# A one-core encoder kernel: plain one-hot products in PSUM, finer background steps in the first mixer, 68 early tiles

## The chip, the cores and the metric

The kernel runs on one core of one Trainium2 chip. The metric is device time in microseconds of one execution. Before the change the median of three runs is 3347.67 us (3344.97 to 3349.91).

## The reference, cut to what matters

512 tokens of width 1024 pass through two layers. Layer 0 has an mLSTM mixer with 8 heads, layer 1 a stick-breaking attention with 16 heads; after each mixer comes a PEER expert feed-forward. Every sub-layer is normed, shifted and scaled by vectors that come from a condition c, and its result is gated by another such vector:

```python
sh1, sc1, g1, sh2, sc2, g2 = jnp.split(ada_mod(c, ada_w[layer], ada_b[layer]), 6, axis=-1)
h = modulate(rmsnorm(x, norm_mix_g[layer]), sh1, sc1)
...
x = x + g1[:, None, :] * y
h = modulate(rmsnorm(x, norm_ffn_g[layer]), sh2, sc2)
x = x + g2[:, None, :] * peer_ffn(h, peer_w_q[layer], peer_sub_keys[layer], peer_u[layer], peer_v[layer])
```

In the feed-forward each token picks, for each of 8 heads, 16 of 16384 experts (an expert is a pair of two keys out of 128 each), with softmax weights g. It then adds up g * gelu(u . x) * v over the 128 picks:

```python
u = jnp.take(peer_u, expert, axis=0)
act = jax.nn.gelu(jnp.einsum('thkd,td->thk', u, xb).astype(jnp.float32), approximate=False)
vv = jnp.take(peer_v, expert, axis=0)
return jnp.einsum('thk,thkd->td', (g * act).astype(xb.dtype), vv)
```

## The kernel before, in words

**Products.** All large products take float32 operands split into a rounded high part and a remainder (`whi`, `wlo`), three matmuls for one. ScalarE casts the high part, VectorE or GpSimd subtracts.

**The feed-forward (`peer`, line 763).** 128 tokens gather their experts' rows by indirect DMA. For the other 384 tokens the kernel goes through all 16384 experts densely, in 128 tiles of 128 experts. A tile needs the activations gelu(U x), which are 24 matmuls of 384 columns, the matrix G of routing weights for that tile, and the product with V, which is 18 matmuls of 512 columns.

**The placement stage (lines 808 to 984).** It makes G from one-hot vectors, chunk by chunk: 8 tokens make a chunk (`CHUNK`), and the 384 tokens of a layer make 48 chunks, in two layers 96. For each chunk `expand` (line 919) lets VectorE write the one-hot columns `oA` (line 930) and `oB` (931), GpSimd scale `oA` by the high part of the weight (`oH`, line 933, 8 operations of 128 columns), and three engines share the scaling by the remainder (`oL`): tokens below `SHARE[0]` on GpSimd (935), from there to below `SHARE[1]` on ScalarE (`scale`, 942), the rest on VectorE (937). One chunk later `place` (944) multiplies, two float16 matmuls per token (950 and 951), 16 per chunk, into a PSUM tile `gps` that holds four tokens interleaved, so that one token's 128 results are 4 elements apart. ScalarE copies each four tokens to `stg` (953), whence G goes to DRAM. Between the placements TensorE works on activation tiles that are wanted later: the first `NPRE` = 64 tiles are done here (`early_acts`, 836, matmuls in 845), their count per half chunk given by `share` (962). The first 16 of these stay in SBUF, the rest go to DRAM (855). In this stage the order of TensorE, VectorE and ScalarE is the program's (864).

**The value stage (lines 986 to 1083).** For each of 128 tiles it adds the product with V (1080). Tiles that were not early get their activations here (`act`, 1027, matmuls in 1034). Groups of four early and four late tiles alternate (991 to 997). The gathers of the 128 tokens (1002 to 1022), 257 steps, are spread over the late tiles' steps (1025 and 1073): 64 - 1 - 3 = 60 steps.

**The first mixer (`mlstm`, line 254) and the background sums.** The vectors from c are sums over 8 weight tiles of 512 KB each: VectorE multiplies a tile by c and adds it (`part`, lines 148 and 152), and at the end TensorE adds across partitions by 8 matmuls of one column (`end`, 157). Those not wanted at once are `background` steps. `tick(n)` (89) runs n of them; before each it issues the load of the next one. The tiles live in `araw`, 2 buffers, loaded on the SP queue, which also loads the projections' weights (103). A sum's `end` comes six steps after its last part, or right behind it where `flush` is set (169); in the first mixer this holds for the fourth and for the last sum. The steps run two at a time in the projections (lines 348 and 369) and four at a time at the start of each of the 8 heads (436). A head has four score blocks; for each, VectorE, ScalarE and GpSimd make the weights (`weights_of`, 414, result P of line 428), TensorE fills in with some matmuls of the output gate (`gate`, 442, line 382) and multiplies by P (446). In the heads the order of TensorE alone is the program's (432); elsewhere in the mixer, and on the other engines in the heads, the order is the scheduler's.

Of the kernel before, what the change touches and what calls it, by code (L numbers as in the profile page):

```python
# [7 lines left out]
F32 = mybir.dt.float32  # L8
# [4 lines left out]
AF = mybir.ActivationFunctionType  # L13
# [14 lines left out]
NSUB = ND // 32  # L28
NGRP = NA // 4
GROW = NSUB * 128 + 32  # L30
NPRE = 64
RCHUNK = 2.0
KEEP = (4, 4)
DEPTH = 3
SHARE = (2, 4)
GSTEP = (6, 5, 4, 3, 2)
HLB = 3
CHUNK = 8
# [11 lines left out]
def body(tc, nc, A, ctx):  # L50
# [38 lines left out]
    def tick(n):  # L89
        for _ in range(min(n, len(background))):  # L90
            load, run = background.pop(0)
            load()
            if background:
                background[0][0]()
            run()

    def split(hi, lo, src, eng):
# [37 lines left out]
    def ada(j, ap, pool, ring=None, flush=False):  # L135
        def start():
            acc[j] = pool.tile([128, 1024], F32, name="acc", bufs=2)

        raw = {}

        def load(k):
            if k not in raw:
                raw[k] = ring[k % len(ring)] if ring else pool.tile([128, 1024], F32, name="araw", bufs=2)
                nc.sync.dma_start(raw[k], ap[k])

        def part(k):
            if k == 0:
                first = V.tensor_scalar(acc[j], raw[k], csil[:, 0:1], None, op0=OP.mult)
                if j in (2, 8):
                    tc.keep_in_program_order(first)  # L150
            else:
                V.scalar_tensor_tensor(acc[j], raw[k], csil[:, k:k + 1], acc[j], op0=OP.mult, op1=OP.add)

        def end():
            ps = pp()
            for k in range(KD):
                PE.matmul(ps[:, k:k + 1], acc[j][:, k * 128:(k + 1) * 128], ones[:, 0:1], start=True, stop=True)
            V.tensor_tensor(mod[:, j], ps[:, 0:KD], adab[:, j], op=OP.add)
            if j in scale_of:
                gain(scale_of[j], j)  # L160

        def step(k):
            def run():
                if k == 0:
                    start()
                part(k)
                if k == KD - 1:
                    ends.append(end)
                if ends and (k == 5 or k == KD - 1 and flush):
                    ends.pop(0)()  # L170
            return lambda: load(k), run
        return [step(k) for k in range(KD)]
# [81 lines left out]
    def mlstm():  # L254
        with ExitStack() as st:
# [138 lines left out]
            with tc.tile_pool(name="mlps", bufs=1, space=PSUM) as pq:  # L394
                dn = pq.tile([64, T], F32, name="dn")

                def totals(h, *srcs):
                    for i, src in enumerate(srcs):
                        PE.matmul(dn[32 * i:32 * i + 32], oc[:, 32 - h:64 - h], src, start=h == 0, stop=h == 7)

                def rows_of(h):
                    rb = pq.tile([128, T], F32, name="rb", bufs=2)
                    PE.matmul(rb, sel[:, h], rw, start=True, stop=True)
                    return rb

                def scores_of(h, I):
                    e, r0 = h // 2, 64 * (h % 2)
                    rows = slice(r0, r0 + 64)
                    sp = pq.tile([128, T], F32, name="sp", bufs=2)
                    PE.matmul(sp[:, I * 128:T], qk[4 + e][rows, I * 128:I * 128 + 128], qk[e][rows, I * 128:T],  # L410
                              start=True, stop=True)
                    return sp

                def weights_of(h, I, rb, sp):
                    lo, s = I * 128, slice(I * 128, T)
                    Dm = wk.tile([128, T], F32, name="Dm")
                    for J in range(I, 4):
                        js = slice(J * 128, (J + 1) * 128)
                        n = pairs.index((I, J))
                        if I == J:  # L420
                            V.tensor_scalar(Dm[:, js], rb[:, js], cols[:, n, h:h + 1], 0.0, op0=OP.add, op1=OP.min)
                            S.activation(Dm[:, js], Dm[:, js], AF.Exp)
                        else:
                            S.activation(Dm[:, js], rb[:, js], AF.Exp, bias=cols[:, n, h:h + 1])
                    G.affine_select(Dm[:, lo:lo + 128], Dm[:, lo:lo + 128], pattern=[[1, 128]], compare_op=OP.is_ge,
                                    fill=0.0, base=0, channel_multiplier=-1)
                    Pm = wk.tile([128, T], F32, name=f"P{min(I, 1)}")
                    V.scalar_tensor_tensor(Pm[:, s], sp[:, s], 0.125, Dm[:, s], op0=OP.mult, op1=OP.mult)
                    return Pm

                ms = ExitStack()
                ms.enter_context(tc.manual_schedule(engines={nc.tensor.engine}))
                rb = rows_of(0)
                late = None
                for h in range(8):
                    tick(4)
                    pn = pq.tile([128, T], F32, name="pn")
                    sps = [scores_of(h, 0), scores_of(h, 1)]
                    P0 = None
                    for I in range(4):  # L440
                        Pm = weights_of(h, I, rb, sps[I])
                        gate(GSTEP[I])
                        if I == 0 and late:
                            totals(h - 1, *late)
                        s = slice(I * 128, T)
                        PE.matmul(pn[:, s], vt[I][:, h * 128:(h + 1) * 128], Pm[:, s], start=I == 0, stop=I == 3)
                        if I < 2:
                            sps.append(scores_of(h, I + 2))
                        if I == 0:
                            P0 = Pm  # L450
                        else:
                            G.tensor_tensor(P0[:, s], P0[:, s], Pm[:, s], op=OP.add)
                    if h < 7:
                        rb = rows_of(h + 1)
                    gate(GSTEP[4])
                    S.copy(num[h], pn)
                    sq = wk.tile([128, T], F32, name="cv")
                    S.activation(sq, num[h], AF.Square)
                    late = P0, sq
                gate(4)  # L460
                totals(7, *late)
                gate(24 * 8)
                ms.close()
                rows2 = keep.tile([8, 2, T], F32, name="rows2")
                S.activation(rows2[:, 0], dn[0:8], AF.Abs)
                V.tensor_copy(rows2[:, 1], dn[32:40])
                pd = pp()
                for i in range(2):
                    for J in range(4):
                        PE.transpose(pd[:, i * 32 + J * 8:i * 32 + J * 8 + 8], rows2[:, i, J * 128:(J + 1) * 128], ident[0:8, 0:8])  # L470
                dm = keep.tile([128, 4, 8], F32, name="dm")
                V.tensor_tensor(dm.rearrange("p a b -> p (a b)"), pd[:, 0:32], cols[:, 10:14].rearrange("p a b -> p (a b)"), op=OP.max)
                V.scalar_tensor_tensor(dm, dm, EPS, dm, op0=OP.mult, op1=OP.mult)
                d2 = dm.rearrange("p a b -> p (a b)")
                V.scalar_tensor_tensor(d2, pd[:, 32:64], 1.0 / 128.0, d2, op0=OP.mult, op1=OP.add)
                V.tensor_scalar(dm, dm, 1e-37, None, op0=OP.max)
                S.activation(dm, dm, AF.Sqrt)
                V.reciprocal(dm, dm)
                for h in range(8):
                    S.activation(og[h], og[h], AF.Sigmoid)  # L480
                    V.scalar_tensor_tensor(num[h], og[h], hg[:, h:h + 1], num[h], op0=OP.mult, op1=OP.mult)
# [281 lines left out]
    def peer(l):  # L763
# [3 lines left out]
        with ExitStack() as st:  # L767
# [19 lines left out]
            with ExitStack() as s1:  # L787
# [156 lines left out]
                def place(s, c, stg, oB, oA, oH, oL, gl, o):  # L944

                    for j in range(CHUNK // 4):
                        gps = pq.tile([128, 128, 4], F32, name="gps", bufs=2)
                        for i in range(4):
                            n = 4 * j + i
                            PE.matmul(gps[:, :, i], oB[:, n], oH[:, n], start=True, stop=False)  # L950
                            PE.matmul(gps[:, :, i], oB[:, n], oL[:, n], start=False, stop=True)  # L951
                        k = c * CHUNK + 4 * j
                        S.activation(stg[:, :, k:k + 4], gps, AF.Copy, scale=1.0 / GSCALE)
                    if c == 32 // CHUNK - 1:
                        nc.scalar.dma_start(Gd[:, :, s * 128:(s + 1) * 128].rearrange("g p c -> p g c"),
                                            stg.rearrange("p (g a) t -> p g (a t)", a=4))
# [245 lines left out]
```

## Time and profile before

| | us |
|---|---|
| median of three runs | 3347.67 |
| the profiled execution, its time | 3354.71 |
| its span on the core | 3353.0 |
| first mixer's heads, from to | 195 to 350 |
| placement stages | 580 to 900, 2220 to 2550 |
| value stages | 900 to 1700, 2550 to 3350 |

The span is what the profiler saw of the core; the time has 1.7 us around it. Times in the rows are from the start of the span. PE is TensorE's matmuls, PEld its weight loads, DVE is VectorE, ACT ScalarE, POOL GpSimd, SP the queue that issues loads. A matmul's duration is not its share of the engine, since matmuls overlap: the distance from one start to the next is.

### The profile page before, as it was taken

What the parts mean: (1) busy time and instruction counts of PE and PEld (TensorE: products, weight loads), DVE (VectorE), ACT (ScalarE), POOL (GpSimd) and SP (SyncE); (2) the same over time, 40 slices, a digit from 0 to 9 for tenths busy, and PEclk for the clock granted to TensorE, in tenths of its full rate; (3) what the DMA queues carried; (4) which work ended last, traced back from release to release, by engine and by line L of the source; (5) the groups of instructions that cost most, each with busy time, mean ns of one, the idle gap of its engine ahead of it and who ended that gap; (6) DMA issues with size and microseconds to landing.
All of it is one profiled execution on the core that took longest, in us unless ns stands there. A gap on an engine that the chain in (4) does not pass through costs nothing. (4 is left out here: it accounts for less than half of the span.)

```text
span 3353.0 us, 45548 instructions
## 1 busy us (share of the span) xinstructions
PE 3209.6 (96%) x16160; PEld 2752.9 (82%) x16160; DVE 2468.6 (74%) x4656; ACT 1341.9 (40%) x2090; POOL 1641.2 (49%) x1801
## 2 busy tenths in 40 slices
PE   6879998999999999999989999989999999999999
PEld 5744787999988888888866657889998888888887
DVE  6854379776588888888875483896775887887888
ACT  4234333555433333333342463345553333333332
POOL 3422442888734434444453455258884444344443
PEclk9977999999999999999989899999999999999999
DMA  5653222666799999999956102236668999999997
GB/s 196 210 192 107 69 78 76 189 191 205 219 359 332 336 357 332 341 356 340 335 180 214 57 1 78 70 120 197 206 200 289 338 336 355 335 341 351 338 352 275
DMA packets 306580, 792.41 MB, mean 236 GB/s; under 512 B 24368, under 2 KB 135216, under 8 KB 306352
## 3 DMA queue, kind: packets, MB, share of 16 engines
q1 hardware_dynamic: 120112, 451.83, 38.1%
q0 software_dynamic: 73728, 268.47, 22.0%
q10 hardware_dynamic: 112512, 69.21, 7.1%
q8 instruction: 126, 2.06, 0.2%
q14 instruction: 102, 0.84, 0.1%
HBM read 718.12 MB, written 71.30 MB: 235 GB/s over the span
## 5 line engine op out<-in xcount | busy, mean ns | idle before, releaser
L98 ACT CAST whi<-wraw 128x1024 fp32r<-128x1024 f32 x481 | 504.1, 1050 | 665.2 <-PE y L1080 245.4
L1004 POOL DMA_INDIRECT rows<-in_v,pidx x256 | 360.8, 1409 | 426.0 <-DVE yt L1022 385.9
L99 DVE TENSOR_TENSOR wlo<-wraw,whi 128x1024 fp32r<-128x1024 f32 x384 | 469.3, 1222 | 130.1 <-ACT whi L98 129.1
L1004 POOL DMA_INDIRECT rows<-in_u_rows,pidx x256 | 319.0, 1246 | 483.8 <-DVE rows L1011 427.1
L933 POOL TENSOR_SCALAR oH<-oA,gh 128x128 f16<-128x128 f16 x768 | 440.7, 588 | 229.1 <-DVE oA L930 190.2
L1080 PE MATMUL y<-wlo,Wh 128*128 128x512 f32 x1536 | 475.8, 391 | 0.0
L1080 PE MATMUL y<-whi,Wl 128*128 128x512 f32 x1536 | 472.8, 390 | 0.0
L1080 PE MATMUL y<-whi,Wh 128*128 128x512 f32 x1536 | 430.8, 392 | 8.5 <-ACT Wh L98 5.5
L99 POOL TENSOR_TENSOR wlo<-wraw,whi 128x1024 fp32r<-128x1024 f32 x97 | 246.1, 2541 | 333.0 <-ACT whi L98 332.6
L845 PE MATMUL ua<-hh,wlo 128*128 128x384 f32 x1024 | 349.7, 342 | 10.9 <-DVE wlo L834 10.8
L845 PE MATMUL ua<-hh,whi 128*128 128x384 f32 x1024 | 349.5, 341 | 1.4 <-ACT sf L804 1.4
L845 PE MATMUL ua<-hl,whi 128*128 128x384 f32 x1024 | 348.4, 340 | 0.0
L1022 DVE SCALAR_TENSOR_TENSOR yt<-rows,uw,yt 128x1024 f32<-128x1024 f32 x254 | 327.1, 1288 | 25.1 <-DMA rows<-in_v,pidx 24.1
L1034 PE MATMUL pp<-hh,wlo 128*128 128x384 f32 x1024 | 344.0, 336 | 0.7 <-DVE wlo L99 0.7
L1034 PE MATMUL pp<-hl,whi 128*128 128x384 f32 x1024 | 343.2, 335 | 0.0
L1034 PE MATMUL pp<-hh,whi 128*128 128x384 f32 x1024 | 343.0, 335 | 0.0
L1080 PEld LDWEIGHTS y<-wlo,Wh 128*128 128x128 f32 x1536 | 289.4, 188 | 61.4
L1080 PEld LDWEIGHTS y<-whi,Wh 128*128 128x128 f32 x1536 | 287.6, 188 | 62.8 <-ACT Wh L98 6.1
L1080 PEld LDWEIGHTS y<-whi,Wl 128*128 128x128 f32 x1536 | 288.0, 188 | 58.4
L1011 DVE SCALAR_TENSOR_TENSOR rows<-rows,htok 128x1024 f32<-128x1024 f32 x256 | 309.4, 1219 | 8.1 <-DMA rows<-in_u_rows,pidx 7.8
L115 PE MATMUL pp<-hh,whi 128*128 128x512 f32 x584 | 235.4, 411 | 21.9 <-ACT cbuf L353 9.2
L834 DVE TENSOR_TENSOR wlo<-wraw,whi 128x1024 fp32r<-128x1024 f32 x128 | 159.2, 1248 | 111.2 <-ACT whi L826 111.0
(296 smaller groups left out, 6090.4 us busy)
## 6 DMA issues: line engine op xcount, KB each, us to landing
wraw<-in_u SPq DMA_DIRECT2D x256, 512.0 KB, 4.7
wraw<-in_v SPq DMA_DIRECT2D x256, 512.0 KB, 6.5
g<-stg ACTq DMA_DIRECT2D x24, 2048.0 KB, 10.7
gb<-g SPq DMA_DIRECT2D x64, 768.0 KB, 7.7
araw<-in_ada_w SPq DMA_DIRECT2D x80, 512.0 KB, 4.0
spd<-ga ACTq DMA_DIRECT2D x96, 192.0 KB, 3.7
ga<-spd SPq DMA_DIRECT2D x24, 768.0 KB, 11.0
wraw<-in_peer_q SPq DMA_DIRECT2D x32, 512.0 KB, 3.6
```

Of the source, the lines that this page charges most:

```text
L98: S.copy(hi, src)
L99: eng.tensor_tensor(lo, src, hi.bitcast(F32), op=OP.subtract)
L115: PE.matmul(ps, a[:, ws], b[k][:, t0:T], start=n == 0, stop=n == 3 * KD - 1)
L834: V.tensor_tensor(p[2], p[0], p[1].bitcast(F32), op=OP.subtract)
L845: PE.matmul(ps, p[:, ws], q[k][:, T0:T], start=n == 0, stop=n == 3 * KD - 1)
L933: G.tensor_scalar(oH[:, n], oA[:, n], gh[:, o + n:o + n + 1], 1.0, op0=OP.mult, op1=OP.mult)
L1004: tc.keep_in_program_order(G.indirect_dma_start(out=r, out_offset=None, in_=rows, in_offset=bass.IndirectOffsetOnAxis(ap=pidx[:, n:n + 1], ...
L1011: V.scalar_tensor_tensor(r, r, 1.0, htok, op0=OP.mult, op1=OP.mult, accum_out=uw[:, n:n + 1])
L1022: V.scalar_tensor_tensor(yt, r, uw[:, n:n + 1], yt, op0=OP.mult, op1=OP.add)
L1034: PE.matmul(ps[:, :ND], p[:, ws], q[k][:, T0:T], start=n == 0, stop=n == 3 * KD - 1)
L1080: PE.matmul(y[t][d], wa[:, ts], vb[:, d * 512:(d + 1) * 512], start=n == 0 and i == 0, stop=n == NA - 1 and i == 2)
```

## The change

It turns the PSUM tile so that each token's 128 results are contiguous, and ScalarE reads it across; GpSimd scales one remainder column of a chunk instead of two, VectorE five instead of four; 68 tiles are early instead of 64; `tick` issues the loads of two steps ahead, with three buffers; and the heads' four background steps go to the four score blocks, one each, behind the block's weights. One group of four activation tiles more per layer goes through DRAM.

```diff
-NPRE = 64
+NPRE = 68
...
-SHARE = (2, 4)
+SHARE = (1, 3)
...
             load()
-            if background:
-                background[0][0]()
+            for ahead, _ in background[:2]:
+                ahead()
             run()
...
-                raw[k] = ring[k % len(ring)] if ring else pool.tile([128, 1024], F32, name="araw", bufs=2)
+                raw[k] = ring[k % len(ring)] if ring else pool.tile([128, 1024], F32, name="araw", bufs=3)
...
                 for h in range(8):
-                    tick(4)
...
                         Pm = weights_of(h, I, rb, sps[I])
+                        tick(1)
                         gate(GSTEP[I])
...
-                        gps = pq.tile([128, 128, 4], F32, name="gps", bufs=2)
+                        gps = pq.tile([128, 4, 128], F32, name="gps", bufs=2)
                         for i in range(4):
                             n = 4 * j + i
-                            PE.matmul(gps[:, :, i], oB[:, n], oH[:, n], start=True, stop=False)
-                            PE.matmul(gps[:, :, i], oB[:, n], oL[:, n], start=False, stop=True)
+                            PE.matmul(gps[:, i], oB[:, n], oH[:, n], start=True, stop=False)
+                            PE.matmul(gps[:, i], oB[:, n], oL[:, n], start=False, stop=True)
                         k = c * CHUNK + 4 * j
-                        S.activation(stg[:, :, k:k + 4], gps, AF.Copy, scale=1.0 / GSCALE)
+                        S.activation(stg[:, :, k:k + 4], gps.rearrange("p t a -> p a t"), AF.Copy, scale=1.0 / GSCALE)
```

## Rows read from the trace of the kernel before

**Rows 1.** The page: the span, and TensorE's busy time.

```profile
span 3353.0 us, 45548 instructions
PE 3209.6 (96%) x16160; PEld 2752.9 (82%) x16160; DVE 2468.6 (74%) x4656; ACT 1341.9 (40%) x2090; POOL 1641.2 (49%) x1801
```

**Rows 2.** Windows by stage: projections, heads, 24 placement chunks, value stage.

```profile
core 0: us, PE busy (x) PEld busy (x) DVE busy (x) ACT busy (x) POOL busy (x), PEclk, DMA share, GB/s
112.00:195.00 83.00, 66.38 (x305) 53.18 (x303) 56.53 (x46) 20.17 (x29) 26.68 (x12) 0.87 0.66 217
195.00:350.00 155.00, 141.73 (x417) 75.76 (x417) 73.58 (x106) 60.90 (x126) 49.33 (x62) 0.78 0.38 125
636.40:795.40 159.00, 157.22 (x1035) 151.96 (x1034) 111.20 (x238) 85.33 (x154) 135.38 (x238) 1.00 0.65 202
1000.00:1600.00 600.00, 599.65 (x2904) 528.94 (x2903) 493.24 (x639) 216.28 (x292) 262.39 (x196) 1.00 0.93 344
```

**Rows 3.** Chain that ended last: start, length, work; placement stage, then value stage.

```profile
2442.85 4.86 PE ua L845 x28
...
2449.48 4.87 PE ua L845 x28
...
2859.28 4.12 PE y L1080 x18
2863.40 4.18 PE pp L1034 x24
```

**Rows 4.** TensorE's timeline, end of one placement: start, duration, engine, line, operation.

```profile
806.04 0.31 PE L950 MATMUL gps<-oH,oB 128*128 128x128 f16 x1
...
806.80 0.31 PE L951 MATMUL gps<-oL,oB 128*128 128x128 f16 x1
806.88 0.42 PE L845 MATMUL ua<-hh,wlo 128*128 128x384 f32 x1
807.13 0.34 PE L845 MATMUL ua<-hh,whi 128*128 128x384 f32 x1
```

**Rows 5.** TensorE's timeline, two other places with small matmuls, at the full clock.

```profile
123.09 0.78 PE L361 MATMUL pp<-ident,cb 8*128 8x8 f32 x10
```

```profile
526.77 0.28 PE L912 MATMUL pp<-identr,hh 128*128 128x128 f32 x1
526.89 0.28 PE L912 MATMUL pp<-identr,hl 128*128 128x128 f32 x1
```

**Rows 6.** Single lines: weight loads of the products and of line 912, min/median/max ns.

```profile
L950 PEld LDWEIGHTS <-oB x768: 96/139/139, 581.2 to 2543.1; 128*128 128x128 f16 x192
```

```profile
L912 PEld LDWEIGHTS pp<-identr,hh x16: 188/192/192, 526.0 to 2170.1; 128*128 128x128 f32 x16
```

**Rows 7.** Groups by line, 24 placement chunks (636.4 to 795.4 us): busy, mean ns, idle before.

```profile
L935 POOL TENSOR_SCALAR oL<-oA,gl 128x128 f16<-128x128 f16 x48 | 30.8, 642 | 0.0
...
L953 ACT ACTIVATE stg<-gps 128x512 f32<-128x512 f32 x48 | 27.7, 595 | 22.0 <-PE gps L951 22.0
...
L937 DVE TENSOR_TENSOR oL<-oA,g 128x512 f16<-128x512 f16 x24 | 10.5, 437 | 13.8 <-PE gps L951 13.8
```

**Rows 8.** Single lines: ScalarE's other reads of PSUM, across and plain, min/median/max ns.

```profile
L546 ACT ACTIVATE rk<-pp,eps x2: 280/284/288, 1851.4 to 1851.6; 128x32 f32<-128x32 f32 x2
```

```profile
L424 ACT ACTIVATE Dm<-rb,cols x48: 348/356/368, 194.0 to 330.3; 128x128 f32<-128x128 f32 x48
```

**Rows 9.** Windows of 25 us in the value stage, columns as in rows 2.

```profile
1175.00:1200.00 25.00, 25.00 (x118) 21.44 (x117) 21.16 (x32) 8.86 (x12) 10.31 (x9) 1.00 1.02 397
1200.00:1225.00 25.00, 25.00 (x129) 22.75 (x128) 19.22 (x28) 8.82 (x12) 10.21 (x8) 1.00 0.81 290
```

**Rows 10.** Waits, 112 to 195 us: who waited for whom, total, times, longest.

```profile
PE pp L157 <- DVE acc L152: 15.6, 2, 12.6
```

```profile
DVE acc L152 <- DMA araw<-in_ada_w: 22.4, 14, 3.1
```

**Rows 11.** The first mixer's heads, 195 to 350 us: a wait, and line 152.

```profile
PE pn L446 <- DVE P L428: 13.3, 8, 4.9
```

```profile
L152 DVE SCALAR_TENSOR_TENSOR acc<-araw,csil,acc x27: 1270/1285/3417, 197.1 to 309.6; 128x1024 f32<-128x1024 f32 x27
...
  DMA araw<-in_ada_w: 12.7, 10
  DMA araw<-in_kv_ada_w: 11.3, 10
```

**Rows 12.** TensorE's timeline at the first head: its longest wait there.

```profile
188.24 1.01 PE L157 MATMUL pp<-ones,acc 128*128 128x1 f32 x4 [12.59 <-DVE acc L152]
```

## The prediction

> **What bounds the kernel now.** I read the page first: matmuls are under way in 96% of the span [rows 1]. That number cannot say what each stage waits for, so the windows by stage come next [rows 2]. In the value stage TensorE is busy 599.65 of 600 us, and over 24 placement chunks 157.22 of 159, both at the full clock: there the end moves with TensorE's work alone. In the first mixer it is otherwise. From 112 to 195 us TensorE is idle for 16.6 us (83 less 66.38), in the heads for 13.3 (155 less 141.73), and the granted clock is 0.78 in the heads: waits count there, not work.
>
> The chain of waits gives the period of a placement chunk: activations start at 2442.85 and again at 2449.48, so 6.63 us, of which 28 activation matmuls take 4.86 [rows 3], 0.174 each. The rest is the 16 one-hot products. The timeline shows their spacing: from 806.04 to 806.80 are 7 starts, 0.109 us each; the activation that follows the last one starts only 0.07 later, though it then takes 0.42 instead of 0.34 [rows 4]. Last I read the waits of the mixer [rows 10 to 12].
>
> **The change part by part.**
>
> *Products written plainly.* There are 96 chunks of 16 products. What a product costs with contiguous results no row shows. From above, it is 0.109, if the writes were never the limit. From below: line 912 also has 128 columns with contiguous results and a start every 0.11 us (526.77 to 526.89) [rows 5], but it loads float32 weights, 192 ns against 139 for the products [rows 6]. If loading sets its pace, a load shorter by 0.053 allows 0.058. Line 361, whose matmuls have 8 columns, makes ten in 0.78 us; without the last one's drawn-out end of about 0.2, nine intervals are 0.064 each [rows 5]. I take 0.070, the step from the last product to the activation, because it is the products' own weights and columns and only the next result goes elsewhere [rows 4]. Fifteen intervals of a chunk fall by 0.039: 0.585 us, and 96 chunks give **-56**. The lower end, 0.058, gives 73 in place of 56; the upper one 0.
>
> The Trainium skill's page "TensorE: Matmul & The Clock Gate", section "Back-to-back issue gap", puts a stream of load and matmul pairs of 128 columns at some 0.081 us each, more than the 0.070 that the row shows at its one place. By it the term would be 40 (15 x 0.028 x 96), an estimate, and the sum below 3296.
>
> *Read across by ScalarE.* 192 copies at 595 ns now [rows 7]. Of reads across PSUM the trace has only line 546: 32 elements in 284 ns; a plain read of 128 takes 356 [rows 8]. Between 128 and 512 plain elements the slope is 0.62 ns each, so 32 would take 296: the read across cost nothing more, which puts a copy at 595, the lower end (a read that is contiguous today can't gain from strides). If all 284 ns were its elements, a copy would be 4.5 us, the upper end. Line 546 steps by pairs, the new read by single elements, so I take something between near the lower end: under 1.2 us. ScalarE is busy 85.33 us in 24 chunks, 3.56 each, against a period of 6.4, so up to 2.0 us per copy hide behind TensorE. Two copies' buffers (`gps`, two) are asked for again a whole chunk later. Cost on the path: 0.
>
> *Shares of the remainder.* GpSimd loses one operation of 642 ns per chunk [rows 7] and goes from 5.64 (135.38 by 24 [rows 2]) to 5.0. VectorE's line goes from four columns to five, 437 to about 546 ns: 4.63 (111.2 by 24) to 4.75. ScalarE keeps two. All lie under 6.4; should the cover go, VectorE would add 0.11 x 96 = 10.
>
> *68 early tiles.* Per layer 96 more activation matmuls in the placement stage, 96 x 0.174 = 16.7, and four times 24 fewer in the value stage, 4 x 4.18 = 16.7 [rows 3]: both stages are TensorE's, so 0 for two layers. The chunk becomes 28.25 + 2 = 30.25 matmuls x 0.174 + 16 x 0.07 = 6.4 us. With them go, per layer, four ScalarE casts and gelus, four remainders on VectorE and four loads on SP, whose queue in that stage holds nothing else, and one more group of activations to DRAM and back (four issues on ScalarE's queue, one load of 768 KB). Hidden under 3.56 and 4.63 of 6.4. In the value stage the 257 gather steps go to 56 late tiles instead of 60, 4.59 per tile instead of 4.28, and the transfers there are at a share of 0.93 to 1.02 [rows 2, 9]. I add **+4** for new short waits.
>
> *Loads two ahead.* VectorE waits 22.4 us for the background tiles from 112 to 195 us [rows 10] and 24.0 in the heads (12.7 + 11.3) [rows 11]: each load is issued when the part two before it is done, and has one part's time to land. Now it has two. The load stands at the same wait in SP's queue (the part before frees the buffer), so the weight loads of line 103 behind it are not held longer, except at the first tick, which issues three in place of two. The price of the third, 512 KB at 217 GB/s [rows 2], is 2.4 us, hidden by three weight buffers.
>
> *Ticks per block.* TensorE's longest wait of the mixer, 12.59 us, stands at the first head [rows 12]: the flushed sum's matmuls wait for VectorE to catch up with all steps so far. In the new order that sum ends in the first head's second block, behind some 4 us of other TensorE work, and VectorE is up to 20 us earlier through the loads. I count 10 of 12.6 as gone. Late next is P: TensorE waits 13.3 us for it in 8 places [rows 11], partly because four parts of 1.285 us and their loads stand ahead of a head's first block. Spread, each part stands between one block's P and the next block's mask: 1.285 us at best and 3.417 at worst [rows 11], in front of what TensorE wants next, and the gate's matmuls cover it. I count 6 of 13.3 as gone: **-16** together. From above the term is -26 and some clock on top; from below, +16 if each of the 32 ticks makes TensorE 0.5 us later than today.
>
> *The second mixer* has the same two loads ahead; TensorE hardly waits there, so 0.
>
> **Sum.** -56 + 4 - 16 = -68. The profiled execution took 3354.71 us, span and 1.7 around it; the sum makes 3286.7 of it. It stands 7.0 above the median of the runs, so **3280** for the median.
>
> **The rivals.**
>
> *The weights pace the products.* Line 912 has contiguous results and float32 moving data, and its spacing is 0.11 all the same [rows 5]. If a float16 load took the array as long, writing plainly gains nothing; the first term is 0 and the time 3336. Against it speak the shorter load [rows 6] and the 0.07 behind the last product. The Trainium skill's page "PSUM — Partial Sum Buffer", section "Specifications (TRN2)", has any non-contiguous access slow matmuls significantly, lines being 8 bytes; by that rule the writes are the limit, and the forecast stands. A third of this rival has no gain in the mixer either: no change. Chance 0.12.
>
> *The value stage runs into the transfers.* In stretches with late tiles the share is 1.02 at 397 GB/s [rows 9]. 0.31 gathers more per tile are 0.16 MB, 0.65 MB for a group of four, 1.7 us at that rate; 15 such groups in two layers make 51 if nothing moves over into the early tiles' stretches, which are at 0.81 and have room. Half of it makes 3305. Chance 0.12.
>
> *ScalarE's read across becomes the bound*, the one that ends slower. The copies then set the chunk's period: 3.56 + 2(s - 0.595). The bound moves to ScalarE from s = 2.0 us. Against the 33.4 us that leave the value stage and the 16 of the mixer the kernel is slower once the period passes 7.14, from s = 2.4. At 2.6 it is 7.57, and 96 x 0.94 - 49 = +41: 3389. For it speaks only that nothing in the trace reads 512 single elements across; line 546 speaks against [rows 8]. Chance 0.06.
>
> **How the numbers follow.** The forecast has 0.70. Its own range runs from 3254 (products at 0.058, -17, and 9 more in the mixer) to 3312 (0.081 and no gain in the mixer). I stretch the upper end to 3322, which takes in the transfers; the weights' rival and ScalarE's, 0.18 together, stay outside. A measurement of this kernel tells about 0.2% from no change, 7 us. Faster: 0.70 + 0.12 + 0.08 = 0.90; within: 0.04; slower: 0.06.
>
> **What would show it.** Right: starts of products 0.06 to 0.08 us apart, a chunk of about 6.4 us, GpSimd at 5.0 per chunk; a value stage shorter by some 17 us with TensorE still busy throughout; no long wait at line 157 at the first head and VectorE's waits for `araw` below 10 us. Wrong: products still 0.109 apart; copies above 2 us with TensorE waiting behind ScalarE or for `gps`; TensorE idle in the value stage behind W or gathered rows; longer waits for P in the heads.

## The result, and the profile after

The changed kernel takes 3297.94 us in the median of four runs (3281.91 to 3300.13), beside 3348.79 for the kernel before on the same chip (four runs, 3344.97 to 3351.21). The ratio is 0.9839, 95% interval 0.9806 to 0.9872: some 54 us less by the ratio and 51 between the medians, inside the range of the prediction and 18 us above its forecast. The profiled execution took 3300.13 us. One of the four timed runs of the variant with five row buffers, below, took 4398.09 us at a granted clock of 0.65, far from its other three, and is left out of that variant's median.

The page first. It answers to [rows 1].

```profile
span 3298.2 us, 45462 instructions
PE 3125.8 (95%) x16160; PEld 2672.1 (81%) x16160; DVE 2465.9 (75%) x4656; ACT 1335.2 (40%) x2092; POOL 1618.2 (49%) x1705
```

The span fell by 54.8 us and TensorE's busy time by 83.8. So work left TensorE, and 29 us of idle time came in. The windows by stage tell where; they answer to [rows 2]. The heads now end at 320.3 us, so the second window ends at 320.5, and the placement window holds chunks of the first layer.

```profile
core 0: us, PE busy (x) PEld busy (x) DVE busy (x) ACT busy (x) POOL busy (x), PEclk, DMA share, GB/s
112.00:195.00 83.00, 73.49 (x323) 57.85 (x322) 67.75 (x62) 21.99 (x35) 35.07 (x17) 0.90 0.78 272
195.00:320.50 125.50, 119.37 (x426) 67.55 (x425) 63.22 (x101) 64.76 (x126) 52.48 (x58) 0.92 0.36 118
600.00:840.00 240.00, 230.01 (x1666) 219.83 (x1666) 175.48 (x375) 131.44 (x240) 193.73 (x330) 0.99 0.71 215
1000.00:1600.00 600.00, 597.66 (x2882) 525.62 (x2882) 494.17 (x625) 214.21 (x289) 265.94 (x194) 1.00 0.93 344
```

What to see: in the heads the granted clock rose from 0.78 to 0.92. The placement stage, full before (157.22 of 159 us), now leaves TensorE idle for 10 of 240. The value stage is nearly as full as it was: idle for 2.3 of 600 us, where it was 0.35.

I cut both traces at the first and last starts of four lines (490, which ends the first mixer; 845 and 951 for the placement; 1080 for the value stage):

| stretch | before | after | difference | predicted |
|---|---|---|---|---|
| start to first 490 | 354.0 | 320.3 | -33.7 | -16 |
| 490 to first 845 | 170.0 | 169.3 | -0.7 | 0 |
| placement, two layers | 377.6 + 376.9 | 367.8 + 366.7 | -20.0 | -56 + 33.4 = -22.6 |
| value stage, first to last 1080 | 780.2 + 780.2 | 763.7 + 765.3 | -31.4 | -33.4 |
| TensorE's waits for `yt` behind it | 3.4 | 28.7 | +25.3 | +4 |
| second mixer and its queries, without that wait | 462.5 | 468.7 | +6.2 | 0 |
| the rest | | | -0.5 | 0 |

The sum is -54.8. Two terms came out almost as predicted, though the first hides two errors that cancel. One missed by 18 in favour of the change, one by 21 against it.

**The products.** TensorE's timeline in one placement, its first start and its end, answers to [rows 4].

```profile
797.00 0.23 PE L950 MATMUL gps<-oH,oB 128*128 128x128 f16 x1
...
797.73 0.22 PE L951 MATMUL gps<-oL,oB 128*128 128x128 f16 x1
797.79 0.22 PE L950 MATMUL gps<-oH,oB 128*128 128x128 f16 x1
797.85 0.22 PE L951 MATMUL gps<-oL,oB 128*128 128x128 f16 x1
797.87 0.42 PE L845 MATMUL ua<-hh,whi 128*128 128x384 f32 x1
```

The 16 starts run from 797.00 to 797.85: 0.057 us each, against 0.109. The next activation starts 0.02 behind the last product, where it was 0.07. The single lines answer to [rows 6] and to the second row of [rows 7] (engine, operation, count, min/median/max ns).

```profile
L950 PEld LDWEIGHTS <-oB x768: 95/98/151, 546.5 to 2492.9; 128*128 128x128 f16 x192
L953 ACT ACTIVATE stg<-gps x192: 585/592/604, 547.2 to 2493.3; 128x512 f32<-128x512 f32 x192
```

A weight load is 98 ns long where it was 139, although the loads themselves were not edited. It is 98 in the run below with the plain products alone and 139 in the one with the products interleaved again, so the length goes with the writes. ScalarE's read across takes 592 ns, against 595.

**The new tail.** At the end of each value stage TensorE now stands still.

```profile
1639.40 0.61 PE L1080 MATMUL y<-whi,Wl 128*128 128x512 f32 x2
1657.99 0.48 PE L1098 MATMUL pp<-ident,yt 128*128 128x128 f32 x1 [17.97 <-DVE yt L1022]
...
3276.20 0.61 PE L1080 MATMUL y<-whi,Wl 128*128 128x512 f32 x2
3287.49 0.47 PE L1098 MATMUL pp<-ident,yt 128*128 128x128 f32 x1 [10.68 <-DVE yt L1022]
```

`yt` is the gathered tokens' sum: 256 gathers, each followed by one VectorE operation. Before, the last gather was issued 8 and 10 us ahead of the last product (1692.6 against 1700.5, 3332.2 against 3342.6). Now it is issued 10 and 4 us behind it (1649.4 against 1639.6, 3280.7 against 3276.4). The gathers kept their pace of some 3.05 us each, and the stage around them became shorter. What GpSimd waits for, from 1000 to 1600 us (total, times, longest), first before the change, then after it:

```profile
POOL rows L1004 <- DVE rows L1011: 177.4, 85, 5.9
POOL rows L1004 <- DVE yt L1022: 144.9, 83, 5.8
```

```profile
POOL rows L1004 <- DVE yt L1022: 167.3, 94, 9.2
POOL rows L1004 <- DVE rows L1011: 152.3, 75, 5.6
```

For 319.6 of 600 us GpSimd waits until VectorE has freed one of the four row buffers; before, it was 322.3.

**Stalled chunks.** The steady period of a chunk fell from 6.63 to 6.17 us, with 30 or 31 activation matmuls in place of 28, but the mean only from 6.78 to 6.57 (47 periods per layer). In the first layer chunks 21 to 24 (counted from 0) took 7.0, 8.4, 7.6 and 8.5, and 36 to 40 took 8.4, 8.7, 7.4, 6.8 and 7.7. Stalls were there before, in 21 to 24 and 39 to 40; summed above the steady period they were 14 us in two layers, and are 37 now. VectorE's timeline in chunk 22, and TensorE's wait in it:

```profile
689.57 1.31 DVE L744 TENSOR_TENSOR eq<-eq,t 128x2048 f16<-128x2048 f16 x1
690.91 0.74 DVE L746 TENSOR_TENSOR eq<-eq 128x1024 f16<-128x1024 f16 x1
691.69 0.50 DVE L748 TENSOR_TENSOR eq<-eq 128x512 f16<-128x512 f16 x1
692.23 0.69 DVE L751 TENSOR_REDUCE ab<-eq 128x128 f32<-128x512 f16 x1
692.83 1.22 DVE L834 TENSOR_TENSOR wlo<-wraw,whi 128x1024 fp32r<-128x1024 f32 x1
```

```profile
694.10 0.45 PE L845 MATMUL ua<-hh,wlo 128*128 128x384 f32 x1 [1.56 <-DVE wlo L834]
```

ScalarE's cast of that tile ran from 687.81 to 688.86. Its remainder `wlo` then stood behind four operations of the next tile's routing, 3.2 us, since VectorE's order is the program's here; TensorE waited for it.

Chunk 36 stalls in another way. The two chunks as windows, columns as above, then ScalarE's and TensorE's timelines in the second:

```profile
687.27:695.63 8.36, 6.80 (x51) 6.19 (x49) 8.26 (x12) 4.29 (x8) 6.82 (x8) 1.00 0.39 124
779.93:788.31 8.38, 6.33 (x48) 6.04 (x48) 3.74 (x13) 1.81 (x4) 3.57 (x9) 1.00 1.09 315
```

```profile
780.08 6.50 ACTq L855 DMA_DIRECT2D spd<-ga  x1
786.62 1.04 ACT L826 CAST whi<-wraw 128x1024 fp32r<-128x1024 f32 x1 [6.57 <-issue]
```

```profile
788.31 0.22 PE L950 MATMUL gps<-oH,oB 128*128 128x128 f16 x1 [2.05 <-ACT stg L953]
```

VectorE is busy for 3.74 us only. ScalarE stands for 6.50 us in the issue of an early tile's write to DRAM, which takes 0.33 in the median, right behind the 2 MB write of G issued at 778.55; the copies to `stg` come late by that, and TensorE waits 2.05 for them. From chunk 7 on about every fourth chunk has such a long issue, before the change too (2.7 to 5.1 us); in the first layer's chunks 15, 27, 31 and 43 TensorE loses nothing by it.

### The profile page after: what moved, and what is told of

It reads as the page before. It is cut to its first block, busy times and chain, and to the rows that moved or that the text cites. A ratio compares the mean times of both kernels' runs of the same rounds, so it can differ in the third digit from the quotient of the medians.

```text
span 3298.2 us, 45462 instructions
## 1 busy us (share of the span) xinstructions
PE 3125.8 (95%) x16160; PEld 2672.1 (81%) x16160; DVE 2465.9 (75%) x4656; ACT 1335.2 (40%) x2092; POOL 1618.2 (49%) x1705
## 5 line engine op out<-in xcount | busy, mean ns | idle before, releaser
L98 ACT CAST whi<-wraw 128x1024 fp32r<-128x1024 f32 x473 | 495.0, 1050 | 633.4 <-PE y L1080 235.5
L845 PE MATMUL ua<-hh,wlo 128*128 128x384 f32 x1088 | 371.6, 342 | 18.9 <-DVE wlo L834 18.9
L845 PE MATMUL ua<-hh,whi 128*128 128x384 f32 x1088 | 370.6, 341 | 1.4 <-ACT sf L804 1.4
L845 PE MATMUL ua<-hl,whi 128*128 128x384 f32 x1088 | 369.7, 340 | 0.0
L1034 PE MATMUL pp<-hh,wlo 128*128 128x384 f32 x960 | 322.7, 336 | 1.7 <-DVE wlo L99 1.7
L1034 PE MATMUL pp<-hl,whi 128*128 128x384 f32 x960 | 321.9, 335 | 0.0
L1034 PE MATMUL pp<-hh,whi 128*128 128x384 f32 x960 | 321.7, 335 | 0.0
```

The costliest lines, as they stand in the source:

```text
L98: S.copy(hi, src)
L845: PE.matmul(ps, p[:, ws], q[k][:, T0:T], start=n == 0, stop=n == 3 * KD - 1)
L1034: PE.matmul(ps[:, :ND], p[:, ws], q[k][:, T0:T], start=n == 0, stop=n == 3 * KD - 1)
```

## The experiments

Each ran beside the kernel before (3336 to 3356 us in those runs), and ratios are to it. Diffs are against the changed kernel, except for the first.

**One part alone: the products.** The kernel before, with only the PSUM tile turned and read across:

```diff
-gps = pq.tile([128, 128, 4], F32, name="gps", bufs=2)
+gps = pq.tile([128, 4, 128], F32, name="gps", bufs=2)
-PE.matmul(gps[:, :, i], ...)
+PE.matmul(gps[:, i], ...)
-S.activation(stg[:, :, k:k + 4], gps, AF.Copy, ...)
+S.activation(stg[:, :, k:k + 4], gps.rearrange("p t a -> p a t"), AF.Copy, ...)
```

> The kernel before with the plain products and the read across alone (64 early tiles, shares 2 and 4, mixer as before). Mine: the writes were the limit, so products start 0.056 us apart as in the changed kernel, a steady chunk takes 28.25 x 0.174 + 16 x 0.056 = 5.8 us, 96 chunks save up to 79 us; GpSimd at 5.6 of these 5.8 and VectorE's routing take back 15 to 30, so 3285 to 3300, with value stages of 780 us and no wait over 5 us at the transposes that end them. Rival, the gain hangs on the other parts: less than 40 us saved, over 3309.

3320.44 us, ratio 0.9924 (0.9907 to 0.9940): 25 us, not the 56 or more I expected. The steady chunk is 5.83, 0.80 below 6.63, which over 96 chunks is 77 us. But the mean chunk is 6.46 to 6.49: some 60 us of stalls (0.64 x 94), where the kernel before has 14. TensorE's waits from 600 to 820 us; before, the first of them was 1.7 and the others absent.

```profile
PE gps L950 <- POOL oH L933: 4.5, 4, 1.9
PE ua L845 <- DVE wlo L834: 3.2, 4, 1.4
PE gps L950 <- ACT stg L953: 2.3, 3, 1.4
PE gps L951 <- ACT oL L942: 2.0, 5, 0.8
```

VectorE and GpSimd, covered before, are no longer, and the two ScalarE lines make 4.3 of the 12 us. The products' gain hangs in part on the other parts: the run with 64 early tiles, below, differs from this one, outside the mixers, by the shares alone, and its placement stages are 4 us shorter each.

**One part undone: the products interleaved again,** all else changed.

```diff
-gps = pq.tile([128, 4, 128], F32, name="gps", bufs=2)
+gps = pq.tile([128, 128, 4], F32, name="gps", bufs=2)
```

> The changed kernel with the products four elements apart again. Mine: products 0.109 apart, a chunk of 30.25 x 0.174 + 16 x 0.109 = 7.0 us; 68 tiles and shares gain nothing by themselves and the gathers' tail stays (25 us more than before), the mixer's 33 us stay: 3335 to 3350. Rival, the products gave little and the 68 tiles or the mixer the rest: under 3320.

3338.13 us, ratio 0.9969 (0.9953 to 0.9986). A chunk is 6.97 when steady and 7.02 in the mean, with hardly a stall, so the 68 tiles alone fill the chunk again; the tails stay at 18.3 and 10.8. Within the change the products are worth 0.013, some 43 us.

**One part undone: the first mixer's steps as before.**

```diff
-            for ahead, _ in background[:2]:
-                ahead()
+            if background:
+                background[0][0]()
-... name="araw", bufs=3)
+... name="araw", bufs=2)
                 for h in range(8):
+                    tick(4)
...
-                        tick(1)
```

> The changed kernel with the first mixer's old background steps (four at a head's start, one load ahead, two buffers). Mine: the heads end 33 us later, as in the kernel before, everything behind is the same: 3326 to 3336. Rival, half of the 33 comes from elsewhere or is given back later: 3305 to 3318.

3330.07 us, ratio 0.9937 (0.9915 to 0.9958). Line 490 starts at 351.3 again, and the wait at the first head is back in TensorE's timeline:

```profile
189.06 3.57 PE L157 MATMUL pp<-ones,acc 128*128 128x1 f32 x16 [10.67 <-DVE acc L152]
```

The window of its heads, columns as above:

```profile
195.00:351.40 156.40, 142.22 (x437) 75.50 (x435) 76.22 (x116) 65.21 (x134) 51.87 (x64) 0.80 0.38 125
```

The clock is 0.80 as well. The mixer's part is worth about 0.010, 33 us, as much as the table shows and twice what I predicted. Its size varies between executions: in the eight other variants with the new mixer line 490 starts at 312.6 to 316.4, earlier than the 320.3 of the changed kernel's profile, and with the old one at 348.4 to 354.0, so the part is worth 28 to 41.

**Each half of the mixer's part alone.** First the deeper loads, with four steps at the start of a head; then one step per block, with one load ahead and two buffers.

```diff
                 for h in range(8):
+                    tick(4)
...
-                        tick(1)
```

> The changed kernel with four background steps at each head's start again, but loads two ahead and three buffers. Mine: the loads take VectorE's waits for the background tiles away, and with them most of the first head's 12.6 us at line 157; the spread gives the clock and the waits for P in the heads: 12 to 20 us of the mixer's 33 stay, 3311 to 3319. Rival, the loads do it all: 3298 to 3303. Rival, the spread does it all: 3325 or more.

```diff
-            for ahead, _ in background[:2]:
-                ahead()
+            if background:
+                background[0][0]()
-... name="araw", bufs=3)
+... name="araw", bufs=2)
```

> The changed kernel with one background step per score block, but one load ahead and two buffers. Mine: 13 to 21 us of the mixer's 33 stay, 3310 to 3318, with VectorE waiting 20 us or more for the background tiles from 112 to 195 us. Rivals: 3298 to 3303 (the spread does it all) or 3325 and more (the loads do).

3311.36 us, ratio 0.9889 (0.9863 to 0.9915), and 3306.51 us, ratio 0.9873 (0.9853 to 0.9893), the second somewhat under my expectation. Line 490 starts at 326.9 and 326.8, so either half brings 27 of the 33.7 us: they overlap. They do it differently. The two windows of the loads alone:

```profile
112.00:195.00 83.00, 77.59 (x339) 60.12 (x338) 68.93 (x65) 22.12 (x36) 35.77 (x18) 0.92 0.79 277
195.00:327.00 132.00, 123.64 (x405) 68.61 (x404) 61.65 (x98) 64.60 (x126) 50.70 (x58) 0.84 0.34 108
```

The same two of the blocks alone:

```profile
112.00:195.00 83.00, 64.95 (x302) 50.89 (x300) 56.41 (x52) 21.13 (x32) 30.54 (x14) 0.89 0.69 234
195.00:327.00 132.00, 126.69 (x441) 72.25 (x442) 71.14 (x108) 65.60 (x129) 55.92 (x62) 0.89 0.43 137
```

And of the blocks alone a wait from 112 to 195 us (total, times, longest):

```profile
PE pn L446 <- DVE P L428: 17.4, 1, 17.4
```

With the loads alone VectorE catches up before the heads, and TensorE works 77.59 of the 83 us. With the blocks alone VectorE is still late, the wait merely passes from line 157 to the first P (17.4 us), but the heads behind it run at 0.89 and end as early.

**One part undone: 64 early tiles.**

```diff
-NPRE = 68
+NPRE = 64
```

> The changed kernel with 64 early tiles. Mine: the waits for the last gathered rows at the ends of the value stages (18.0 and 10.7 us) come from 68 tiles, whose late tiles have 4.59 gathers each; with 64 they fall below 5. The value stages go back to 780 us (33 us more in two), the placement stages lose 15 to 33: the sum lies between 3273 and 3295. Rival, the tail has another cause (the earlier start, the order of groups): it stays at 10 us or more and the time is 3298 or above.

3284.05 us, ratio 0.9820 (0.9799 to 0.9841). The value stages are 781.2 and 778.3 us again, the placement stages 357.7 and 358.7, and the last gathers are issued 8 us ahead of the last product. All that is left of the tail:

```profile
PE pp L1098 <- DVE yt L1022: 1.0, 1, 1.0
```

The intervals of this run and of the changed kernel overlap, but the medians are 14 us apart (the ratios 6) and the profiled spans 19.6, of which 6.4 lie in the first mixer, which the edit doesn't touch. The stages tell more: with 68 tiles the placement stages are 18.1 us longer together, the value stages 30.5 shorter, and the waits for `yt` 27.7 more, a loss of 15. What the 68 tiles take from the value stages, the gathers' tail gives back nearly whole, and the placement stages pay for them.

**Two attempts at the tail by the program's order.** Gather steps counted over all tiles of the value stage, not the late ones alone; then the steps spread over 52 late tiles instead of 56.

```diff
-total, spread, step = len(todo), NA - NPRE - 1 - DEPTH, 0
+total, spread, step = len(todo), 2 * (NA - NPRE) + NPRE - 8 - 2 * DEPTH, 0
...
-step += flat[n + DEPTH] >= NPRE
+step += 1 + (flat[n + DEPTH] >= NPRE)
```

> The changed kernel (68 tiles) with the 257 gather steps spread over all tiles by their time, a late tile counting twice an early one, and done about four tiles before the end. Mine: the late stretches ask for more than the transfers carry and the rest is left for the end; spread evenly the rows come in time, the waits of 18.0 and 10.7 us at the end fall below 5 each and TensorE stays at over 99% in the value stages: 3270 to 3280. Rival, the transfers are at their limit over the whole stage, so TensorE waits inside it instead: 3290 or more.

```diff
-total, spread, step = len(todo), NA - NPRE - 1 - DEPTH, 0
+total, spread, step = len(todo), NA - NPRE - 5 - DEPTH, 0
```

> The changed kernel with the gather steps given to 52 late tiles instead of 56, so that the program issues the last before the last late group. Mine: 4.94 per late tile are still more than the late stretches carry, but the last group's time is left to drain them: the waits at the end fall to under 8 us in all, 3272 to 3285. Rival, the backlog grows with the rate and stays: 3292 to 3302.

Both of my own expectations fell. 3299.85 us, ratio 0.9841 (0.9814 to 0.9869), and 3301.48 us, ratio 0.9837 (0.9803 to 0.9872); the waits for `yt` are 17.7 and 16.6 at their longest, the gathers' pace the same. In these two, where a gather stands in the program doesn't set its time.

**Row buffers.** So I gave the gathers more of them, in both places that use the pool.

```diff
-r = vp.tile([128, D], F32, name="rows", bufs=4)
+r = vp.tile([128, D], F32, name="rows", bufs=6)
```

> The changed kernel with six row buffers for the gathers in place of four. Theory (GpSimd issues a gather only when VectorE has freed one of four row buffers, and that pace, some 3.05 us per gather, is the floor of about 785 us which the shorter value stage ran into): gathers run ahead, the last one is issued before the last product, TensorE's waits for yt of 17.97 and 10.68 us go below 3 us each, and the time falls from 3298 to 3270-3280. Rival (the pace is that of VectorE's own order of row sums among the value stage's work, or of the transfers; more buffers only let rows wait longer): the waits stay at 15-18 and 10-11 us and the time stays at 3293-3302.

3359.63 us, ratio 1.0034 (1.0016 to 1.0052): slower than the kernel before, which neither theory had. The mechanism was right: the gathers run at 2.26 us each in the first layer (577 us for 256; the 2.34 of the next expectation is too high), the last one is issued 237 us before the end, and there is no wait for `yt` over 2 us. But the value stages grew to 809.0 and 812.5. The windows of a stretch with gathers and of one that is mostly without:

```profile
1000.00:1200.00 200.00, 191.50 (x913) 165.36 (x912) 186.94 (x272) 66.45 (x92) 129.69 (x91) 1.00 1.02 400
1400.00:1600.00 200.00, 193.88 (x928) 169.71 (x928) 116.96 (x132) 69.71 (x93) 26.36 (x19) 0.99 0.63 228
```

TensorE's waits from 1000 to 1600 us:

```profile
PE y L1080 <- ACT whi L98: 14.5, 8, 2.7
PE y L1080 <- DVE wlo L99: 7.5, 10, 1.6
PE pp L1034 <- DVE wlo L99: 7.2, 9, 1.2
```

TensorE waits 29 us for weight tiles, where the changed kernel waited about 2: half behind ScalarE's casts, half behind VectorE's remainders. The transfers are full (share 1.02), but VectorE, which has an operation for every gather, is nearly full too: 186.94 of 200 us, where it was 164. No run tells the two apart. Either way four buffers had held the gathers to a pace that the stage could bear. Five tell whether the cost comes gradually:

```diff
-r = vp.tile([128, D], F32, name="rows", bufs=4)
+r = vp.tile([128, D], F32, name="rows", bufs=5)
```

> The changed kernel with five row buffers for the gathers, between its four (wait for yt 18 and 11 us, time 3298) and six (no such wait, but gathers at 2.34 us each, a DMA share of 1.00 to 1.02 in the value stages, which grow from 764 to 809-812 us, time 3360). Theory A (the gathers cost nothing until the transfers are full, and four buffers were one too few): gathers at 2.6 to 2.9 us each, share 0.95 to 0.98, no wait for yt over 3 us, value stages 764-772 us, time 3268-3285. Theory B (each step of the gathers' pace delays the weight tiles, as gathers ahead of need take their transfers' place): value stages 780-792 us for a pace of about 2.6 us, time 3300-3325. Either way the wait for yt goes.

3274.61 us, ratio 0.9789 (0.9762 to 0.9816). Value stages 771.3 and 769.0, no wait for `yt` over 2 us, gathers at 2.52 us: theory A, though share and pace are higher than I expected. The window from 1000 to 1400 us:

```profile
1000.00:1400.00 400.00, 394.50 (x1892) 344.48 (x1891) 359.25 (x463) 141.41 (x189) 232.88 (x159) 1.00 0.99 382
```

The share is 0.99 and TensorE loses 5.5 of 400 us. With a fifth buffer the tail is gone for a small price: 28.7 us of waits less, 11.3 us of value stage more, 17 together. The median is 23 us below the change's, or 17 by the ratios, whose intervals overlap a little. The sixth buffer is what costs.

**The stalls of the placement stage.** Routing of the next tile is dealt out by nominal microseconds per chunk; in the changed kernel it falls into the first nine or so of 16 chunks.

```diff
-RCHUNK = 2.0
+RCHUNK = 1.4
```

> The changed kernel with 1.4 us in place of 2.0 us of routing charged per placement chunk, so that the routing of the next tile is spread over nearly all 16 chunks of a tile instead of the first nine or ten. Theory (a chunk of about 6.2 us stalls where VectorE has more than that to do: in the changed kernel chunks 21 to 24 and 37 to 40 hold 3.0 to 4.9 us of routing and 7.7 to 9.1 us of VectorE work, while chunks 9 to 12, 25 to 29 and 41 to 46 hold no routing): the stalled chunks go, the mean chunk falls from 6.55-6.59 to 6.2-6.35, the placement stages become 10-17 us shorter each; as the gathers' chain still ends the value stages at its own pace, most of it shows in the time: 3265-3285. Rival (the stalls are made by the 2 MB write of the background every four chunks, which delays the U tiles whatever VectorE does): stalls stay where the writes are, the mean chunk stays at 6.45 or more, time 3288-3300.

3290.17 us, ratio 0.9824 (0.9792 to 0.9856); the intervals overlap, and the profile has to decide. The placement stages are 361.4 and 363.2, 3.5 to 6.4 shorter, less than I expected. The mean chunk is 6.45 to 6.49, between the two expectations. Chunks 21 to 24, stalled before, now take 6.2 to 6.3, and the stalls stand in chunks 26 to 28 and 40 to 43, with two operations of 1.26 us in one chunk. Chunks 22 and 26 of this run:

```profile
679.25:685.60 6.35, 6.35 (x51) 6.19 (x49) 5.82 (x14) 5.89 (x10) 6.35 (x10) 1.00 0.47 139
704.12:711.34 7.22, 6.53 (x51) 6.25 (x49) 7.12 (x11) 4.00 (x7) 7.22 (x8) 1.00 0.49 169
```

Most stalls went with the routing; a 2 MB write of G follows every fourth chunk in either kernel. VectorE is busy 7.12 of 7.22 us in the stalled chunk, and GpSimd throughout. So the write alone does not make a stall, but it is not cleared: the long issues on ScalarE are here as well, 3.1 to 7.6 us each, and chunk 36 of the changed kernel shows that one can stall TensorE without VectorE. So I spread the heavy operations too, and took 64 tiles, which four buffers can bear:

```diff
-NPRE = 68
-RCHUNK = 2.0
+NPRE = 64
+RCHUNK = 1.5
...
-            yield 1.1
+            yield 2.0
...
-            yield 1.1
+            yield 2.0
```

> The changed kernel with 64 early tiles, 1.5 us of routing charged per placement chunk and the four routing operations of some 1.26 us charged 2.0 us each, so that no chunk holds two of them. Theory (with the products short, a chunk's length is set by what VectorE has to do in it, and the stalls are the chunks in which 3 us and more of routing fall; with 1.4 us they moved to the chunks where two such operations and their sums stood together, 4.7 us): no chunk holds over about 3 us of routing, the mean chunk falls from the 6.37 to 6.39 us of the run with 64 tiles alone to 5.9-6.1, 13 to 22 us per layer; the value stages stay at 778-781 us with no wait at their end; time 3245-3265, against 3284 with 64 tiles alone. Rival (the mean over the stage sets it: VectorE, GpSimd and the tiles' arrival are nearly full over the whole stage, so that a stall taken away here turns up there): the mean chunk stays at 6.25 or more and the time at 3275-3290.

3264.40 us, ratio 0.9735 (0.9714 to 0.9755), the fastest of all: 2.65% below the kernel before and about 1% below the change. The mean chunk fell from 6.37 and 6.39 to 6.16 and 6.17, the placement stages from 357.7 and 358.7 to 348.4 and 348.8, less than I had set (5.9 to 6.1) though the time is within it. What is left, from 600 to 820 us:

```profile
PE gps L950 <- POOL oH L933: 4.7, 4, 1.9
PE gps L950 <- ACT stg L953: 1.8, 2, 1.2
PE gps L951 <- ACT oL L942: 0.9, 3, 0.4
```

The waits for `wlo` are gone, those for GpSimd's `oH` and for ScalarE are not; which of these two engines limits next was not tried.

## Why the prediction was right, and where it was not

**Products: the mechanism right, the size too small, and a cover overlooked.** The interleaved writes were the limit: turning the tile alone took the steady chunk from 6.63 to 5.83 us, turning it back alone took it from 6.17 to 6.97. The rival that the weights pace the products at 0.109 is refuted. I took 0.070 us from the one step behind the last product; it is 0.057, just under the lower end of 0.058. In the steady chunk the term was 77, not 56. The Trainium skill's page "TensorE: Matmul & The Clock Gate", section "Back-to-back issue gap", gives 0.081 us for a stream of such pairs; the trace disagrees, at 0.057. Its 0.056 for a single gap, which it says such a stream exceeds, is what the stream here keeps.

But I then said that 3.56 to 5 us of other engines' work hide under a chunk of 6.4. That compares means. Routing makes VectorE's load uneven: in the changed kernel 8.26 us in chunk 22, 3.74 in chunk 36, and a stall in one is not made up in the next. Of the 43.4 us that the shorter steady chunk allows in the placement stages (76.8 less 33.4 for the tiles) 20.0 arrived; the other 23 are added stalls (37 us in place of 14). That the stage came out 3 us from my -22.6 is luck: two errors that cancel. The runs with other routing charges show the routing as one cause, by moving and then shrinking the stalls.

**Read across: right. Shares: worth something, by another way than I said.** The read takes 592 ns, no cost; ScalarE's copies as the bound are refuted. TensorE does wait 2.4 us for `stg` from 600 to 840 us, and 2.05 of them stand behind the long issue of the early tile's write in chunk 36. I had counted those issues as hidden. GpSimd did not get to 5.0 us per chunk but to 5.3 (193.73 of 240 us, 6.57 a chunk): the remainder operation that is left takes 845 ns there in the mean, in place of 642. I put the shares at 0; the two runs with 64 tiles, with the old shares and the new, differ by 8 us in the placement stages.

**68 tiles: the failed step.** I wrote "I add +4 for new short waits" and looked at the transfers' share, and at the number of gather steps per tile. The value stage gave the 31 us. But it also shelters a second chain, the 256 gathers with four row buffers, some 780 us long (256 x 3.05), and before the change that chain had only 8 to 10 us to spare. Taking 16 us from each stage left it uncovered: 28.7 us of waits in place of 3.4. The trace of before held it, in GpSimd's waits for VectorE at the gathers and in the last gather's start; none of my steps used them. The rival "the value stage runs into the transfers" named the right stage with the wrong mechanism: the share stayed at 0.93 while the four buffers throttled the gathers. With six the share was 1.02 and the stages grew, as that rival has it, but VectorE was nearly full as well.

**Mixer: right in mechanism, half in size.** Waits went much as counted. The 12.59 us of [rows 12] at the first head's sum are gone, though 5.72 turn up at its first P:

```profile
187.78 2.08 PE L446 MATMUL pn<-P,vt 128*128 128x512 f32 x2 [5.72 <-DVE P L428]
189.79 1.22 PE L410 MATMUL sp<-qk,qk 64*128 64x256 f32 x2
190.94 3.57 PE L157 MATMUL pp<-ones,acc 128*128 128x1 f32 x16
```

With them TensorE's waits for P are 10.1 us, so of the 25.9 that I set out from 15.8 went. VectorE's waits for background tiles fell from 22.4 to 9.6 up to 195 us and from 24.0 to 1.3 in the heads, and TensorE's idle time in the two windows fell from 29.9 to 15.6, 14 us against my 16. The other 19 go with the clock, 0.78 to 0.92 in the heads, which I named only as something on top of the upper end. In every run of the mixer's parts fewer waits and a higher clock came together; the clock was not changed by itself. Idle time alone does not tell the clock: the loads alone leave less of it in the two windows (13.8 us) than the whole change, with 0.84 in the heads.

**The sum.** -68 against -54.8: the mixer 18 better, the tail 21 worse, the second mixer 6 worse, the rest together 3 worse.

**Open.** What holds ScalarE in the long issues was not tried. Nor is it known where the 6 us in the second mixer come from. Its attention heads take 107.5 us in place of 101.3, and the granted clock of their first 50 us is 0.76 instead of 0.83. Eight of the variants show it, among them the one with the old mixer; the products alone, either half of the mixer alone and six buffers don't. No part of the change sets it by itself. Nor was a run made with five buffers and spread routing together.

## What to carry to other kernels

When a stage gets shorter, list every chain that merely fits inside it, with its last start and its slack; the one that is 10 us from the end becomes the end. Compare cover chunk by chunk, not as a mean over the stage, and even out an engine's load before counting on it. A small pool of buffers can be a throttle that protects the rest of its stage: widen it by one and measure, since the second step here cost 85 us.

## What the runs showed that I had not expected

Contiguous float16 products of 128 columns, each with weights of its own, start 0.057 us apart at the full granted clock, and the rows of their weight loads shrink from 139 to 98 ns with the writes alone. A read of 512 PSUM elements across costs ScalarE the same as a plain one (592 against 595 ns). Gathers at 2.26 us each in place of 3.05 took the transfers from a share of 0.93 at 343 GB/s to 1.02 at 400, and VectorE from 164 to 187 busy us of 200 (1000 to 1200 us); TensorE then lost some 8 of 200 us in weight tiles that came late. An issue of a transfer on ScalarE's queue, 0.33 us in the median, took up to 6.5 us right behind a 2 MB write, with ScalarE standing still.
